# Small row loads on another queue, and a new order and PSUM tile in the first expert block of a streaming-encoder kernel

## The chip, the cores and the metric

The kernel runs on one core of one Trainium2 chip. Its metric is the time in microseconds that the device needs for one execution. Five engines work side by side and wait for one another by semaphores: TensorE (PE; its weight loads are shown apart as PEld), VectorE (DVE), ScalarE (ACT), GpSimd (POOL) and SyncE (SP), which only issues DMAs here. A suffix q (PEq, SPq) marks an engine's instructions that are not counted as busy: branches, loads of registers, DMA issues.

## The reference

For 512 tokens of width 1024, the reference does a LayerNorm, a token mixer (one projection, a gated MLP over blocks, a gated DeltaNet, a merge), a second LayerNorm, and then a mixture of 32 experts, behind which a third LayerNorm stands. The part that the change touches is the mixture:

```python
grp = argmax(softmax(x @ w_rg + b_rg))            # 1 of 4 groups
top_v, top_i = top_k(le, 2)                       # 2 of the group's 8 experts
gate = p_grp * softmax(top_v)
def expert_block(args):
    xb, e = args
    hb = silu(xb @ w1[e]) * (xb @ w3[e])
    return hb @ w2[e]
out = zeros.at[tok].add(y * gate)
h = layer_norm(DEEPNORM_ALPHA * h + out)
```

How many tokens an expert gets depends on the inputs, so the kernel learns it only while it runs.

## The kernel before, in words

Everything up to the router is one long stretch of TensorE work (projections in three passes of split float32). The router places every token: `place(t)` (L1279) runs for four tiles of 128 tokens, its products `cps` count the tokens of each expert, and its products `sps` (L1318) sort them. `sort` (L1325) turns these into indices. `units` (L1475) makes `cnti` from the counts, three integers for each expert, with three comparisons on `cps`, two operations and a cast (L1488). Before the change `units` is called in `place` for the last tile, between the operations that lead to `oh`.

**The experts.** The class `Experts` (L1517) streams the weights of 32 experts in an order that `ord` gives, 6 MB each: four chunks of 1 MB for `w1` and `w3` together and two for `w2`. `run` (L1555) makes a list `steps` of these chunks, and `load(n)` issues the next n of them by `load_big` (L465, the DMA at L472) on SyncE's queue into 17 buffers `raw` in turn; the first block's first chunk is put 14th in the list and goes into a tile of its own, `once`. Of the list, 18 chunks are issued ahead. Then three are issued after the first block's up products, four after each later block's, and two after each block's down products. Each waits until the readers of its buffer's last content are done, and for the semaphore lane that it gets: DMA issues from SyncE and ScalarE share eight lanes, DMAHW0 to 7, in the order of the program, those from GpSimd have others, DMASW0 to 7, and a DMA waits until the lane's last one has landed.

**A block.** Per expert, `up` (L1762) forms x @ w1 and x @ w3. It has a small part, `up(b, None)`, 32 rows `xs` with the weights' columns in four quarters, and large parts `up(b, 0)` and `up(b, 1)` of 64 rows each, in halves of the columns. Its loop over k takes eight slices of 128, two in each chunk, thus k0 and k1 read the first chunk, k2 and k3 the second. The large parts stand under `If` on the count (more than 32, more than 96), the second under the first. All products land in one PSUM tile `u` (L1537), whose last third is the small part's (`self.end`, L1538). `gate` (L1772) makes h = silu(u1) * u3, ScalarE's activation (L1783) and VectorE's product (L1784). `turn` (L1786) transposes h, `down` (L1797) multiplies with `w2`, `store_y` copies the result into `once` and GpSimd scatters it to `y_dram` (L1812). Blocks whose experts are known to be short have the small part alone (`short`). `n` (L1643) loads a count from `cnti` into a register of one engine (L1647) and keeps it.

**The first block** has code of its own, `first` (L1651), since its tokens come straight from the router. `run` first asks `If(n(0) > NA)` (L1600), NA being 64. Then `first` does the small products k0 to k3, the large parts' first half under `If(n > 32)` (L1663) and `If(n > 96)` (L1665), k4 and k5, the second half, then `gate(0, 0)` for the large part (L1670) and k6 and k7. If the count is over 64, the small rows were not the right ones; they are then copied by `tail_rows` and all small products are done again (L1672). The small part's gate follows in `run`, by `gate(b, 1)`.

**The tail's rows.** `Tail` prepares the last LayerNorm while experts run. At block 8 it calls `load_rows` (L1005): GpSimd clears `rx` (L1012), ScalarE's queue issues three DMAs of four rows each into it (L1014), GpSimd clears `rp` (L1015). Behind that GpSimd issues two gathers (L1918). `split_rows` (L1020) begins with a cast of `rx` on ScalarE (L1023).

## Time and profile before

| | |
|---|---|
| time, median of 3 runs | 1171.09 us (1170.65 to 1171.74) |
| profiled execution | 1168.46 us |
| its span | 1166.7 us |
| busy PE / DVE / ACT / POOL | 1030.9 / 631.0 / 367.4 / 214.5 us |
| mean granted clock of TensorE | 0.953 |
| bytes that the DMAs moved | 268.35 MB |

The profile is of one execution, which took 2.63 us less than the median of the runs, and its span is 1.8 us shorter than its own time. A row of a timeline gives the start in us, the duration in us, engine, line and operation, the tile written and the tile read, a count, and in brackets the idle time ahead of it with what ended it. Rows that belong together are put into one, so x16 is sixteen instructions. A row of waits gives the waiting queue, its releaser, the total in us, how often, and the longest. Windows give the busy time of each engine in a stretch. The granted clock is TensorE's, 1.00 being full. DMA share is the mean busy share of the core's 16 DMA engines, and a stream without gaps reads slightly over 1.

### The profile page before, as it was taken

How to read it: one execution, taken by the hardware profiler on the slowest of the kernel's cores; microseconds unless marked ns; L12 is line 12 of the kernel's file. 1: busy time of each engine (PE TensorE's matmuls, PEld its weight loads, DVE VectorE, ACT ScalarE, POOL GpSimd, SP SyncE). 2: the span in 40 equal slices, each digit the busy share in tenths (PEclk: the TensorE clock that was granted, in tenths of full speed). 3: DMA queues.
4: the chain of work that ended last, by engine and by line, in shares of the span. 5: the costliest groups of instructions: out<-in, count | busy, mean ns of one | idle time of the engine just before them, and what ended most of it. 6: DMA issues, size and time to landing. Idle time of an engine off the chain costs nothing. (4 is left out here: it accounts for less than half of the span.)

```text
span 1166.7 us, 18941 instructions
## 1 busy us (share of the span) xinstructions
PE 1030.9 (88%) x7046; PEld 683.4 (59%) x7046; DVE 631.0 (54%) x1420; ACT 367.4 (31%) x803; POOL 214.5 (18%) x288
## 2 busy tenths in 40 slices
PE   5999999999999999999999977797788787878754
PEld 4888788877777777777887733343334443333321
DVE  8475444477678776863585744353234433222256
ACT  6343356444544554544532121112111111010110
POOL 3010100132212222120100112223121222121110
PEclk9999999999999999999999989899899999998955
DMA  5412432611121121111737589998999999999996
GB/s 215 151 70 78 161 106 91 235 55 55 56 72 56 54 73 55 54 56 54 287 123 315 201 330 406 394 391 338 408 367 409 393 409 383 417 388 408 414 418 253
DMA packets 56138, 268.35 MB, mean 230 GB/s; under 512 B 10795, under 2 KB 15179, under 8 KB 32216
## 3 DMA queue, kind: packets, MB, share of 16 engines
q1 hardware_dynamic: 44400, 246.96, 55.2%
q0 software_dynamic: 9008, 14.82, 3.8%
q10 hardware_dynamic: 2616, 5.04, 1.2%
q8 instruction: 73, 1.20, 0.4%
q14 instruction: 41, 0.34, 0.1%
HBM read 273.74 MB, written 21.00 MB: 253 GB/s over the span
## 5 line engine op out<-in xcount | busy, mean ns | idle before, releaser
L275 PE MATMUL psi<-hTh,hi 128*128 128x512 f32 x448 | 183.8, 412 | 0.0
L275 PE MATMUL psi<-hTh,lo 128*128 128x512 f32 x448 | 179.9, 402 | 0.3 <-DVE lo L275 0.3
L275 PE MATMUL psi<-hTl,hi 128*128 128x512 f32 x448 | 179.7, 402 | 0.0
L1784 DVE TENSOR_TENSOR h<-h,u 128x128 f32<-128x128 f32 (+2 forms) x33 | 17.9, 542 | 250.6 <-ACT h L1783 245.1
L275 DVE TENSOR_TENSOR lo<-raw,hi 128x1024 fp32r<-128x1024 f32 x74 | 92.5, 1250 | 75.1 <-ACT hi L275 74.9
L1769 PE MATMUL u<-raw,xs 128*32 128x256 f32 x1296 | 88.9, 413 | 36.3 <-DMA raw<-in_w 22.6
L275 ACT CAST hi<-raw 128x1024 fp32r<-128x1024 f32 x74 | 77.4, 1046 | 107.3 <-PE psi L275 89.9
L275 PEld LDWEIGHTS psi<-hTl,hi 128*128 128x128 f32 x448 | 84.2, 188 | 20.6 <-issue 3.0
L275 PEld LDWEIGHTS psi<-hTh,hi 128*128 128x128 f32 x448 | 84.2, 188 | 20.2 <-issue 3.3
L275 PEld LDWEIGHTS psi<-hTh,lo 128*128 128x128 f32 x448 | 84.4, 188 | 18.4 <-issue 1.9
L1783 ACT ACTIVATE h<-u 128x128 f32<-128x128 f32 (+2 forms) x33 | 15.8, 480 | 243.1 <-PE u L1769 127.3
L1769 PEld LDWEIGHTS u<-raw,xs 128*32 128x32 f32 x1296 | 42.5, 116 | 77.9 <-DMA raw<-in_w 25.4
L1769 PE MATMUL u<-raw,x 128*64 128x512 f32 x304 | 72.9, 622 | 9.2 <-PEq L1681 7.1
L1812 POOL DMA_INDIRECT y_rows<-once,itail x28 | 25.3, 903 | 253.4 <-DVE once L1832 220.0
L275 DVE SCALAR_TENSOR_TENSOR acc<-xp,cols,acc 128x512 f32<-128x512 f32 x72 | 54.1, 751 | 5.3 <-ACT acc L275 4.3
L1793 ACT COPY hT<-t 128x128 f32<-128x128 f32 x32 | 8.5, 265 | 153.4 <-PE t L1790 146.6
L1769 PEld LDWEIGHTS u<-raw,x 128*64 128x64 f32 x304 | 23.1, 142 | 52.3 <-issue 50.3
L1832 DVE COPY once<-yz 32x256 f32<-32x256 f32 x112 | 46.7, 417 | 12.7 <-PE yz L1805 5.8
L1805 PE MATMUL yz<-raw,hT 128*32 128x256 f32 x576 | 43.1, 438 | 11.0 <-DMA raw<-in_w 9.1
L275 POOL TENSOR_TENSOR rk<-ssk,mhalf 128x4 f32<-128x4 f32 x8 | 10.0, 1249 | 178.0 <-DVE ssk L275 178.0
L1695 POOL DMA_INDIRECT mh<-h_dram,idx x36 | 35.0, 972 | 40.3 <-issue 26.5
L1805 PE MATMUL y<-raw,hT 128*64 128x512 f32 x160 | 38.0, 620 | 3.5 <-PEq L1681 2.6
(541 smaller groups left out, 1959.7 us busy)
## 6 DMA issues: line engine op xcount, KB each, us to landing
raw<-in_w SPq DMA_DIRECT2D x147, 1024.0 KB
raw<-in_wt SPq DMA_DIRECT2D x73, 512.0 KB
rawl<-in_w SPq DMA_DIRECT2D x22, 1024.0 KB
rawh<-in_w SPq DMA_DIRECT2D x22, 1024.0 KB
raw<-in_wv SPq DMA_DIRECT2D x8, 512.0 KB
y_rows<-zero SPq DMA_DIRECT2D x8, 512.0 KB
rawl<-in_wo SPq DMA_DIRECT2D x3, 1024.0 KB
vt<-in_x SPq DMA_DIRECT2D x4, 512.0 KB
```

Of the source, the lines that this page charges most:

```text
L275: op._ins = getattr(getattr(self.nc, op.attr), op.name)(*map(real, op.args), **{k: real(x) for k, x in op.kw.items()})
L1695: self.nc.gpsimd.indirect_dma_start(out=x, out_offset=None, in_=self.h1_dram, in_offset=bass.IndirectOffsetOnAxis(ap=self.blocks[b][2 + i] ...
L1769: self.nc.tensor.matmul(self.u[q * r:(q + 1) * r, NP if p is None else p, 0:c], x[:, k, r0:r0 + r], self.raw[b, k // 2][:, o:o + c], start ...
L1783: self.nc.scalar.activation(out=h, in_=u[:, :, 0], func=AF.Silu)
L1784: self.nc.vector.tensor_mul(out=h, in0=h, in1=u[:, :, 1])
L1793: self.nc.scalar.copy(out=x[:, n], in_=self.t[1][:, 0:128])
L1805: self.nc.tensor.matmul(y[q * r:(q + 1) * r, 0:c], t[:, i, j * r:(j + 1) * r], self.raw[b, 4 + k // 2][:, o:o + c], start=k == 0, stop=k == 3)
L1812: x = self.nc.gpsimd.indirect_dma_start(out=out, out_offset=bass.IndirectOffsetOnAxis(ap=idx, axis=0), in_=src, in_offset=None, bounds_che ...
L1832: nc.vector.tensor_copy(out=small[:, q], in_=src)
```

## The change

It has four parts. The three row loads of `load_rows` are issued by GpSimd in place of ScalarE. `units` is called in `sort` and no longer in `place`. The small part's products get a PSUM tile of their own, `us`, so `u` keeps the large parts only, and `gate` does its two parts as two operations on each engine. And the first block does k0 to k3 ahead of its first question for the count, then k4, loads block 1's counts, and does k5, the large part's gate, k6 and k7. The products done again for a count over 64 are k0 to k4 and stand inside the first half's `If`; the `k == end` of a redone k1 only closes a group ahead of them.

```diff
@@ load_rows
-            nc.scalar.dma_start(out=self.rx[32 * i:32 * i + 4], in_=self.a["rows"][R_L1G:R_L2B + 1, :])
+            nc.gpsimd.dma_start(out=self.rx[32 * i:32 * i + 4], in_=self.a["rows"][R_L1G:R_L2B + 1, :])
@@ place
-        if t == NT - 1:
-            a = self.eq.rearrange("p a b -> p (a b)").bitcast(F32)[:, 0:3 * E].rearrange("p (a b) -> p a b", a=3)
-            self.units(W, self.cps[:, NT], self.cnti, made, a)
@@ sort
+        a = self.eq.rearrange("p a b -> p (a b)").bitcast(F32)[:, 0:3 * E].rearrange("p (a b) -> p a b", a=3)
+        self.units(self.W, self.cps[:, NT], self.cnti, self.made, a)
@@ Experts.__init__
-        self.u = ps.tile([128, NP + 1, 512], F32, name="u")
-        self.end = self.u[:, NP]
+        self.u = ps.tile([128, NP, 512], F32, name="u")
+        self.end = ps.tile([128, 512], F32, name="us")
@@ run
         if clear:
+            self.up(0, None, range(0, 4))
             with self.tc.If(self.n(0) > NA):
                 self.s[0]["z"] = self.turn_late(0)
...
-                self.gate(b, 1 if clear and b == 0 else None)
+                self.gate(b, (1,) if clear and b == 0 else (1, 0))
@@ first
         self.s[0]["x"] = self.x[0]
+        up(0, None, range(4, 5))
+        self.n(1), self.n(1, ET.PE, 1)
         with If(d() > 32):
             self.affine(self.x[0], slice(0, NA), self.own(0))
             with If(d() > NA):
-                self.affine(self.x[0], slice(NA, NB), self.s[0]["z"], 3)
+                self.affine_late(0, self.s[0]["z"])
         self.affine(self.xs[1], slice(0, 32), self.own(1), 2)
         self.affine(self.x[1], slice(0, NA), self.own(1))
-        up(0, None, range(0, 4))
-        for h, ks in enumerate((range(4, 6), range(6, 8))):
+        for h in range(2):
             with If(n > 32):
+                if h == 0:
+                    with If(n > NA):
+                        up(0, None, range(1, 2), 1)
+                        up(0, None, range(0, 5))
                 up(0, 0, h)
                 with If(n > 96):
                     up(0, 1, h)
-            if h:
-                self.gate(0, 0)
-            up(0, None, ks)
-        with If(d() > NA):
-            self.tail_rows(0)
-        with If(n > NA):
-            up(0, None)
+            if h == 0:
+                up(0, None, range(5, 6))
+        self.gate(0, (0,))
+        up(0, None, range(6, 8))
@@ gate
-        self.nc.scalar.activation(out=h, in_=u[:, :, 0], func=AF.Silu)
-        self.nc.vector.tensor_mul(out=h, in0=h, in1=u[:, :, 1])
+        for part in (1,) if self.short(b) else parts:
+            if part:
+                h, u = self.s[b]["h"][:, n - 1], self.end[:, 0:256].rearrange("p (w n) -> p w n", w=2)
+                u, w = u[:, 0], u[:, 1]
+            else:
+                h = self.s[b]["h"][:, 0:n - 1]
+                u = self.u.rearrange("p a n -> p (a n)").rearrange("p (a w n) -> p a w n", a=n - 1, w=2)
+                u, w = u[:, :, 0], u[:, :, 1]
+            self.nc.scalar.activation(out=h, in_=u, func=AF.Silu)
+            self.nc.vector.tensor_mul(out=h, in0=h, in1=w)
```

Three places show how it moves instructions. In the rows below, names such as `raw_5447` are the buffers, and brackets name what an instruction waits for by semaphore lane.

The first place is the start of the first block on TensorE. Before, from the last sorting product to k3 (`once` holds the first chunk, `raw_5447` the second):

```order
L1318 MATMUL sps<-wt,oh 128x32
L1692 UNCONDITIONAL_BRANCH
L1647 TENSOR_LOAD cnti
L1600 COMPARE_AND_BRANCH
L1728 MATMUL y_5463<-ident,mh 128x96 x5
L1728 MATMUL y_5464<-ident,mh 128x96 x3
L1600 UNCONDITIONAL_BRANCH x2
L1692 UNCONDITIONAL_BRANCH
L1655 UNCONDITIONAL_BRANCH
L1769 MATMUL u<-once,xs_4776 32x256 x8
L1769 MATMUL u<-raw_5447,xs_4776 32x256 x8
```

The same place now, to k4 (`raw_5448` is the third chunk):

```order
L1316 MATMUL sps<-wt,oh 128x32
L1768 MATMUL us<-once,xs_4776 32x256 x8
L1768 MATMUL us<-raw_5447,xs_4776 32x256
L1695 UNCONDITIONAL_BRANCH
L1768 MATMUL us<-raw_5447,xs_4776 32x256 x7
L1648 TENSOR_LOAD cnti
L1601 COMPARE_AND_BRANCH
L1731 MATMUL y_5463<-ident,mh 128x96 x5
L1731 MATMUL y_5464<-ident,mh 128x96 x3
L1601 UNCONDITIONAL_BRANCH x2
L1695 UNCONDITIONAL_BRANCH
L1768 MATMUL us<-raw_5448,xs_4776 32x256 x4
```

The sixteen products of k0 to k3 moved ahead of the load of the count and its branch, and k4 stands behind the branch.

The second place is the end of the first block on TensorE. Before, from k6 to the first question of block 1 (`raw_5449` is the fourth chunk):

```order
L1769 MATMUL u<-raw_5449,xs_4776 32x256 [waits DMAHW3_49,DVE_49]
L1769 MATMUL u<-raw_5449,xs_4776 32x256 x7
L1670 UNCONDITIONAL_BRANCH
L1672 COMPARE_AND_BRANCH
L1769 MATMUL u<-once,xs_4776 32x256 [waits DVE_49]
L1769 MATMUL u<-once,xs_4776 32x256 x7
L1769 MATMUL u<-raw_5447,xs_4776 32x256 x8
L1769 MATMUL u<-raw_5448,xs_4776 32x256 x8
L1769 MATMUL u<-raw_5449,xs_4776 32x256 x8
L1672 UNCONDITIONAL_BRANCH
L1672 UNCONDITIONAL_BRANCH [waits PE_49]
L1647 TENSOR_LOAD cnti
```

The same place now, again from k6:

```order
L1768 MATMUL us<-raw_5449,xs_4776 32x256 [waits DMAHW3_49]
L1768 MATMUL us<-raw_5449,xs_4776 32x256 x7
L1750 COMPARE_AND_BRANCH
L1731 MATMUL y_5463<-ident,mh 128x96 [waits DMASW2_49,DMASW3_49,PE_49,Activation_49]
L1731 MATMUL y_5463<-ident,mh 128x96 x4
L1731 MATMUL y_5464<-ident,mh 128x96 [waits Activation_49]
L1731 MATMUL y_5464<-ident,mh 128x96 x2
```

The wait for VectorE (the large part's gate) at k6 is gone, and so is the redo of all small products behind it; block 1's late rows (under its own `If`) come next.

The third place is block 8, where the rows are loaded. Before, on ScalarE, from block 7's gate to block 8's and the cast of `rx`:

```order
L1783 ACTIVATE h<-u 128x640 [waits PE_49]
L1793 COPY hT<-t_4775 128x128 [waits PE_49,Activation_49]
L1795 COPY hT<-t_4774 128x512 [waits DVE_49,PE_49]
L1014 DMA rx<-in_rows 4x1024 [waits DMAHW2_49,Pool_49]
L1014 DMA rx<-in_rows 4x1024 [waits DMAHW3_49]
L1014 DMA rx<-in_rows 4x1024 [waits DMAHW5_49]
L1783 ACTIVATE h<-u 128x128 [waits PE_49]
L1023 CAST rp<-rx 96x1024 [waits DMAHW3_49,DMAHW5_49,DMAHW2_49,Pool_49]
```

The same loads now, on GpSimd, between a scatter, a gather, and the tail's gathers:

```order
L1812 DMA y_rows<-once,itail 1024x1024 [waits DMASW2_49,DVE_49]
L1698 DMA mh<-h_dram,idx 64x1024 [waits DMASW3_49,DMASW1_49,PE_49]
L1012 MEMSET rx 96x1024
L1014 DMA rx<-in_rows 4x1024 [waits DMASW4_49,Pool_49]
L1014 DMA rx<-in_rows 4x1024 [waits DMASW5_49]
L1014 DMA rx<-in_rows 4x1024 [waits DMASW6_49]
L1015 MEMSET rp 128x1024
L1918 DMA lgate<-gd_dram,lidx_5491 128x2 [waits DMASW7_49]
L1918 DMA x_5471<-h_dram,lidx 128x1024 [waits DMASW0_49,DVE_49]
```

The loads left ScalarE, where block 8's gate (128x128) stood behind them, and stand in GpSimd's queue between the two memsets, on its lanes. What that does to the weight loads' lanes on SyncE, before:

```order
L472 DMA raw_5447<-in_w 128x2048 [waits DMAHW0_49,PE_49]
L1681 UNCONDITIONAL_BRANCH
L1683 UNCONDITIONAL_BRANCH
L472 ISA
L472 DMA raw_5448<-in_w 128x2048 [waits DMAHW1_49,PE_49]
L472 ISA
L472 DMA raw_5449<-in_w 128x2048 [waits DMAHW2_49,PE_49]
```

And the same three loads now:

```order
L472 DMA raw_5447<-in_w 128x2048 [waits DMAHW5_49,PE_49]
L1684 UNCONDITIONAL_BRANCH
L1686 UNCONDITIONAL_BRANCH
L472 ISA
L472 DMA raw_5448<-in_w 128x2048 [waits DMAHW6_49,PE_49]
L472 ISA
L472 DMA raw_5449<-in_w 128x2048 [waits DMAHW7_49,PE_49]
```

The load into `raw_5449` waited for lane DMAHW2, the one that a row load on ScalarE had taken; now the lanes of the weight loads follow one another without a load of another engine between them.

More of the change, by code (lines that the diff above doesn't have):

```diff
@@ L1733, in affine_late @@
         self.affine(self.x[b % 2], slice(NA, NB), zs, 3)
-        self.tail_rows(b)
-    def tail_rows(self, b):
         self.nc.vector.tensor_copy(out=self.xs[b % 2], in_=self.x[b % 2][:, :, ds(self.n(b, ET.DVE, 2), 32)])
@@ L1760, in place, with up @@
         return (4, 0, 32) if p is None else (2, 64 * p, 64)
-    def up(self, b, p, h=None):
+    def up(self, b, p, h=None, end=KD - 1):
         x, (n, r0, r) = self.xs[b % 2] if p is None else self.s[b]["x"], self.place(p)
@@ L1768, in up, with gate @@
                 o = k % 2 * 1024 + q * c
-                self.nc.tensor.matmul(self.u[q * r:(q + 1) * r, NP if p is None else p, 0:c], x[:, k, r0:r0 + r],
-                                      self.raw[b, k // 2][:, o:o + c], start=k == 0, stop=k == KD - 1)
-    def gate(self, b, part=None):
+                self.nc.tensor.matmul((self.end if p is None else self.u[:, p])[q * r:(q + 1) * r, 0:c], x[:, k, r0:r0 + r],
+                                      self.raw[b, k // 2][:, o:o + c], start=k == 0, stop=k == end)
+    def gate(self, b, parts=(1, 0)):
         n = 2 * NP + 1
-        u = self.u.rearrange("p a n -> p (a n)")[:, 0:256 * n].rearrange("p (a w n) -> p a w n", a=n, w=2)
-        if not part:
+        if "h" not in self.s[b]:
             self.s[b]["h"] = self.hp.tile([128, n, 128], F32, name="h")
-        h = self.s[b]["h"]
-        if self.short(b):
-            part = 1
-        if part is not None:
-            sl = slice(n - 1, n) if part else slice(0, n - 1)
-            h, u = h[:, sl], u[:, sl]
-        self.nc.scalar.activation(out=h, in_=u[:, :, 0], func=AF.Silu)
-        self.nc.vector.tensor_mul(out=h, in0=h, in1=u[:, :, 1])
+        for part in (1,) if self.short(b) else parts:
[8 more added lines that the diff above has]
+            self.nc.vector.tensor_mul(out=h, in0=h, in1=w)
     def turn(self, b):
```

## The prediction

> **What bounds the kernel now.** I read the page's slices first, then the chain of waits in order of time, then windows over the expert stage.
>
> ```profile
> DMA  5412432611121121111737589998999999999996
> ```
>
> From the 24th of the 40 slices (29.2 us each) on, thus from about 670 us, the DMA engines are busy nearly without a break: that is the expert stage, and what stands before it is TensorE's, which no edit touches. The chain shows what the end waits for:
>
> ```profile
> 1126.83 26.65 DMA raw<-in_w
> ...
> 1161.60 1.01 POOL out L1912
> ```
>
> The chain is DMA up to the last weight chunk at 1153.48, then a tail of 13.2 us to the span's end at 1166.7 that no edit touches. So the end moves only if the stream of weights ends earlier, and with its bytes fixed it ends earlier only by holes in it that close. The windows (us, then busy time of PE, PEld, DVE, ACT, POOL with counts, granted clock, DMA share, GB/s) show the holes:
>
> ```profile
> 682.00:688.00 6.00, 1.87 (x22) 0.74 (x20) 2.79 (x17) 1.71 (x4) 1.09 (x2) 0.76 0.48 135
> 688.00:692.00 4.00, 4.00 (x12) 1.31 (x10) 1.17 (x10) 0.00 (x0) 1.80 (x2) 0.51 0.91 334
> 785.00:797.00 12.00, 10.16 (x117) 4.74 (x108) 5.68 (x14) 2.57 (x5) 6.66 (x7) 1.00 0.71 249
> 850.00:870.00 20.00, 16.02 (x125) 6.46 (x119) 5.54 (x13) 1.52 (x4) 6.71 (x7) 0.91 0.95 352
> 870.00:1000.00 130.00, 105.14 (x1116) 50.71 (x1114) 53.21 (x108) 15.47 (x35) 29.93 (x32) 0.97 1.02 399
> ```
>
> A full stream reads 1.02. Against that, **hole A** in block 0 is 6 x (1.02 - 0.48) + 4 x (1.02 - 0.91) = 3.2 + 0.4 = 3.7 us of lost transfer; **hole B** in block 8 is 12 x (1.02 - 0.71) = 3.7 us; **hole C**, 850 to 870, is 20 x 0.07 = 1.4 us; no edit touches what stands there, so it counts for the low end only. After 870 there is none. All that can be won is 3.7 + 3.7 + 1.4 = 8.8 us, and each microsecond won in a hole is one at the end as long as nothing later uses it up. Over 0.2% (2.3 us) is what a measurement of this kernel tells from no change.
>
> **Hole A: the first block's order.** Who holds the weight queue there (SyncE's queue: waits with total, times, longest; then its issues)?
>
> ```profile
> SPq L472 <- PEq L1672: 9.5, 1, 9.5
> ```
>
> ```profile
> 685.47 0.33 SPq L472 DMA_DIRECT2D raw<-in_w  x1
> ```
>
> The load after the first 18 goes into the buffer of the first block's second chunk (k2, k3), and that is given free only at the end of the second `If(n > NA)` (L1672), at 685.47. What TensorE does until then:
>
> ```profile
> 677.88 0.21 PE L1318 MATMUL sps<-wt,oh 128*128 128x32 f16 x2 [0.18 <-DVE oh L1315]
> 679.02 1.07 PE L1769 MATMUL u<-once,xs 128*32 128x256 f32 x16 [0.93 <-PEq L1600]
> 679.88 1.07 PE L1769 MATMUL u<-raw,xs 128*32 128x256 f32 x16
> 681.12 1.07 PE L1769 MATMUL u<-raw,xs 128*32 128x256 f32 x16 [0.17 <-PEq L1663]
> 684.22 1.12 PE L1769 MATMUL u<-raw,xs 128*32 128x256 f32 x16 [2.02 <-DVEq L1670]
> 687.45 5.86 PE L1769 MATMUL u<-raw,x 128*64 128x512 f32 x16 [2.11 <-PEq L1681]
> ...
> 801.02 3.65 PE L1769 MATMUL u<-raw,x 128*64 128x512 f32 x16 [1.19 <-PEq L1681]
> ```
>
> Only products of 32 rows run in block 0, none of 64: its count is small and the large part is skipped. Three idle times stand in a chain: 0.93 for the count, 2.02 because the last small products (k6, k7) write the PSUM tile that the large part's gate still reads, 2.11 for two more counts, which block 1 asks for. The changed order removes them one by one (block 1's counts are loaded ahead of the first `If` now).
>
> (1) *k0 to k3 before the count.* They need only `xs` and the first chunks, not the count, so they follow the sorting products at once: 677.88 + 0.21 = 678.09 as it stands.
>
> ```profile
> 675.04 0.20 DVE L1488 CAST cnti<-oeq 128x96 int32<-128x96 f32 x1
> ```
>
> ```profile
> L1647 PEldq TENSOR_LOAD <-cnti x3: 308/320/492, 677.9 to 686.4; - x3
> ```
>
> The count's six DVE operations, by the row of their last at most 0.20 us each, 1.2 in all, now stand behind `xs` and `oh`. Those come sooner by what six overlapping operations take, for which I put 0.7 us, so k0 starts near 677.4 instead of 679.02. Behind them the count is written by 677.3 + 1.2 = 678.5 at the latest, and after a load of 0.32 to 0.49 it is there by 679.0. The products k0 to k3 last 679.88 + 1.07 - 679.02 = 1.9 us, thus until 679.3. So the later count costs nothing: these products cover it, with 0.3 us to spare. Without the cover TensorE would wait 1.6 us. Pool and DVE load their count later too, but the large parts for which they need it are skipped in block 0.
>
> (2) *Their own PSUM tile.* k6 and k7 no longer wait for the gate of the large part; the 2.02 us go. What follows 679.3 is the count's branch (0.93 at its dearest, as above), k4 (a quarter of the 2.1 us that two groups of 1.07 take: 0.5) and an empty `If` (0.17): it closes near 680.9 instead of 685.47, and nothing that reads the second chunk stands behind it, since the redo with k0 to k4 lies inside. Thus the held load leaves 4.6 us earlier. The next two leave behind k5 and the second `If`, near 681.6, and behind k6 and k7 (1.12), near 682.7. At a full stream's 399 GB/s a chunk (128 x 2048 x 4 bytes, 1.05 MB) lasts 2.6 us, so these three carry it from 682, where the share falls, to 689.8.
>
> (3) *Block 1* needs the gate of block 0's large part, because that reads `u`:
>
> ```profile
> 681.46 1.28 ACT L1359 ACT_TABLE_LOAD   x1
> ...
> 682.86 0.58 ACT L1783 ACTIVATE h<-u 128x512 f32<-128x512 f32 x1
> ```
>
> ```profile
> 683.47 0.69 DVE L1784 TENSOR_TENSOR h<-h,u 128x512 f32<-128x512 f32 x1 [1.41 <-ACT h L1783]
> ```
>
> ScalarE comes to it through its table loads, which stay, so the gate still ends at about 683.47 + 0.69 = 684.2, and that, hidden before behind 687.45, is now what is late: block 1 starts at about 684.1 to 684.2, 3.3 us earlier. If its first half takes 3.65 us, loads go on by 688, before 689.8: the hole closes, 3.7 us, or 3.1 if the first load still comes 0.6 late. If it takes 5.86 us as now, the next load leaves near 690.1; the rows show that a load needs about 2 us until the stream is full (issues from 685.47, still 0.91 after 688), so some 1.7 us of the hole come back: 2.0 us.
>
> Which of the two hangs on the granted clock: 0.76 and 0.51 in the two windows, and 5.86 us there for what took 3.65 at 801. Both lengths are rows of this kernel, and of the 5.1 us of idle time ahead of block 1 about 1.5 stay, so I take the middle of 2.0 and 3.7: **A = 2.8 us**. [...]
>
> **Hole B: the rows' loads.** Around 777 to 792 SyncE's queue (first), ScalarE and GpSimd read:
>
> ```profile
> 776.88 0.33 SPq L472 DMA_DIRECT2D raw<-in_w  x1
> ```
>
> ```profile
> 792.42 2.85 SPq L472 DMA_DIRECT2D raw<-in_w  x4
> ```
>
> ```profile
> 788.78 1.94 ACTq L1014 DMA_DIRECT2D rx<-in_rows  x3
> 790.77 0.28 ACT L1783 ACTIVATE h<-u 128x128 f32<-128x128 f32 x1 [5.88 <-DMA rx<-in_rows]
> 792.76 1.05 ACT L1023 CAST rp<-rx 96x1024 bf16<-96x1024 f32 x1 [1.72 <-DMA rx<-in_rows]
> ```
>
> ```profile
> 787.79 0.97 POOL L1012 MEMSET rx<- 96x1024 f32 x1
> ...
> 791.17 1.00 POOL L1918 DMA_INDIRECT x<-h_dram,lidx  x1 [0.31 <-issue]
> 795.89 0.90 POOL L1812 DMA_INDIRECT y_rows<-once,itail  x1 [3.72 <-DVE once L1832]
> ```
>
> SyncE issues nothing for 15.2 us. By the order of the program its next load waits for semaphore lane DMAHW2 (the quoted rows of the change), which the rows' load on ScalarE holds; that waits for GpSimd's memset of `rx`, which ends at 787.79 + 0.97 = 788.76, and is issued at 788.78. SyncE goes on at 792.42, when they have landed, and issues four loads in 2.85 us: their buffers had long been free. So a transfer of 48 KB, behind a memset that GpSimd reaches late, holds the 1 MB weight loads. After the change the three loads have lanes of GpSimd's own, and the weight loads' lanes follow one another (HW5, 6, 7, 0). The stall goes; what is next is the freeing of buffers by TensorE, which the four loads at once show to be early. I take 3.7 less 0.2 for the first load's own start: **B = 3.5 us**. ScalarE's 5.88 us before its gate L1783 goes too; it lies beside the stream.
>
> *What it adds.* GpSimd issues three DMAs; its own rows show 0.90 to 1.00 us for one, so 3.0 us, against 0.65 each (1.94 / 3) on ScalarE. GpSimd's queue behind them holds the memset of `rp`, two gathers, then block 7's scatter at 795.89, before which it idles 3.72 us: hidden, with 0.7 to spare. The cast at 792.76 waits for `rx`; `rp` is used only after the splits of blocks 9 and 10. If the idle time were gone the 3.0 us would delay the scatter, and through `once` the next block's copies.
>
> **The split gate.** Large and small part are two operations per engine now.
>
> ```profile
> 699.88 0.71 ACT L1783 ACTIVATE h<-u 128x640 f32<-128x640 f32 x1
> ```
>
> ```profile
> L1784 DVE TENSOR_TENSOR h<-h,u 128x640 f32<-128x640 f32 x15 | 12.3, 821 | 178.4 <-ACT h L1783 178.4
> L1784 DVE TENSOR_TENSOR h<-h,u 128x128 f32<-128x128 f32 x17 | 4.9, 288 | 70.8 <-ACT h L1783 65.3 <-issue 5.4
> ```
>
> With the rows above for 128x512 (0.58 on ScalarE, 0.69 on VectorE) and 128x128 (0.28 and 0.29): 0.58 + 0.28 - 0.71 = 0.15 us and 0.69 + 0.29 - 0.82 = 0.16 us more in each of 15 blocks: 15 x 0.31 = 4.6 us in all. They lie beside a full stream, and behind the up products TensorE has the down products of the block before to do. Taken as 0; without that cover it is 4.6.
>
> **Sum.** 2.8 + 3.5 = 6.3 us off the profiled execution's 1168.46 gives 1162.2. The median of the runs lies 2.63 us above that execution, so the forecast is 1171.09 - 6.3 = **1164.8**.
>
> **The rivals.** (a) *Only the rows' part acts*: the first `If` closes as late as before, since the later count, or the gate through its table loads, holds TensorE by some 4 us: 1171.09 - 3.5 = 1167.6. For it speaks the thin cover of 0.3 us in (1); against it that the held load no longer stands behind the gate.
> (b) *Only the first block's part acts*: SyncE is held at 777 by something else that the lane hid: 1171.09 - 2.8 = 1168.3. Against it speak the four loads at once.
> (c) *TensorE becomes the bound later.*
>
> ```profile
> 868.72 0.34 SPq L472 DMA_DIRECT2D rawl<-in_w  x1
> 872.59 0.34 SPq L472 DMA_DIRECT2D rawh<-in_w  x1
> ```
>
> ```profile
> 820.12 1.94 PE L1769 MATMUL u<-rawh,xs 128*32 128x256 f32 x16 [2.59 <-DMA rawh<-in_w]
> ```
>
> At 868.72 to 872.59 SyncE waits 3.5 us for buffers and the stream stays full, so at least 3.5 us were queued. A stream 6.3 us ahead of an unmoved TensorE would run dry for 6.3 - 3.5 = 2.8 us, or 4.8 with a load's 2 us start: 1167.6 to 1169.6. Against it: at 820.12 TensorE itself waits 2.59 us for a weight, so it moves forward with the stream.
> (d) *It doesn't do what it says*: other waits of the same length stand behind both: 1171.1.
> (e) *Slower: GpSimd's queue.* Its DMAs on plain rows are not in the trace at this place. The price decides: the three must last over 3.7 (idle) + 6.3 (gained) + 2.3 (the bound) = 12.3 us, 4.1 each; at 5 us each the scatter of block 7 is 11.3 us late, `once` with it, the copies, TensorE's next products and the buffers: 15 - 3.7 - 6.3 = 5 us slower, 1176.1. The rows of 0.90 to 1.00 speak against it. [...]
>
> **How the numbers follow.** Both holes close 0.60 (1164.8); (a) 0.14; (b) 0.08; (c) 0.07, its range lying on both sides of the bound at 1168.75, so 0.03 faster and 0.04 the same; (d) 0.06; (e) 0.05. Faster: 0.60 + 0.14 + 0.08 + 0.03 = 0.85; the same 0.10; slower 0.05. The low end is all three holes, 1171.09 - 8.8 = 1162.3, rounded down to 1162.0 for the spread of the runs; the high end takes in (a) and (b), 1168.3, and the half of (c) up to 1168.8. Left out are (d), (e) and the other half of (c), 0.15.
>
> **What would show it.** Right: the first load after the 18 leaves near 681; k6 and k7 follow without the 2.02; block 1 starts near 684; no gap of SyncE from 777 to 792; DMA share 1.0 in both stretches; the last weight chunk lands near 1147. Clock: 3.65 or 5.86 us for block 1's first products tells A's size. Wrong: a wait of TensorE on `cnti` at 678, a weight load still behind a semaphore of `rx`, rows' loads over 3 us each on GpSimd, or a new hole between 800 and 875 with SyncE waiting for TensorE.

## The result and the profile after

The changed kernel takes 1162.51 us in the median of six runs (1161.37 to 1166.76); the kernel before, run beside it, takes 1170.92 (six runs). The ratio is 0.9941 with a 95% interval of 0.9923 to 0.9959, that is 6.9 us less (4.8 to 9.0), where 6.3 were forecast (the medians alone lie 8.4 us apart). A second set of six runs gave a median of 1163.32 and a ratio of 0.9950 (0.9935 to 0.9966), 5.9 us less. Two runs of kernels below, one of b_clear_five (2527 us) and one of a_ask_first (2012 us), took 1.7 to 2.2 times as long as all the others and are left out of the ratios.

The two profiled executions differ by less, 1168.46 against 1165.03 us, and this must be cleared first. Windows of the kernel before, far ahead of anything that the change touches:

```profile
500.00:600.00 100.00, 97.19 (x510) 77.51 (x509) 61.88 (x108) 47.64 (x89) 13.12 (x18) 1.00 0.42 149
```

The same window of the changed kernel:

```profile
500.00:600.00 100.00, 97.18 (x497) 77.15 (x496) 58.18 (x104) 46.10 (x87) 12.10 (x18) 0.97 0.42 148
```

The mean granted clock was 0.97 in place of 1.00, with the same code. The mean hides a short stretch at half clock:

```profile
531.60:538.20 6.60, 6.60 (x23) 4.86 (x23) 0.00 (x0) 0.78 (x3) 0.00 (x0) 0.50 0.24 79
```

That is 6.6 x (1 - 0.50) = 3.3 us lost, and by that this execution comes late to the place of the change. The last router operation that both order alike (L1284) is the mark from which to compare. Before, on VectorE:

```profile
672.93 0.19 DVE L1284 TENSOR_TENSOR M<-mk 128x32 bf16<-128x32 f32 x1
```

And after, with the count's cast further down:

```profile
676.23 0.19 DVE L1284 TENSOR_TENSOR M<-mk 128x32 bf16<-128x32 f32 x1
...
681.13 0.21 DVE L1488 CAST cnti<-oeq 128x96 int32<-128x96 f32 x1
```

The mark lies 3.30 us later. From the mark to the span's end it is 1166.7 - 672.93 = 493.8 us before and 1163.2 - 676.23 = 487.0 after, 6.8 us less, which agrees with the runs. The changed kernel's profile in the second set (after_again) has its mark at 672.80, without that stretch, and 1161.1 - 672.80 = 488.3 us behind it, 5.5 less. Two executions of one kernel thus differ by 1.3 us behind the mark. Times are set against this mark where two kernels are compared, unless they are given as they stand in the rows.

The chain of waits still ends in the stream of weights (DMA from 1123.86 for 25.61 us), and goes on:

```profile
1149.47 0.04 issue
1149.51 1.98 PE us L1805 x16
```

The last chunk lands 1149.47 - 676.23 = 473.24 us behind the mark, before it was 1153.48 - 672.93 = 480.55, 7.3 us later. The tail grew by half a microsecond, as the last products now take 1.98 us, where they took 1.11 (granted clock 0.50 for 1.00). The windows over the stream:

```profile
682.00:688.00 6.00, 2.73 (x40) 0.87 (x32) 3.49 (x10) 4.55 (x9) 2.07 (x2) 1.00 0.97 351
688.00:692.00 4.00, 3.50 (x10) 1.21 (x12) 2.68 (x21) 0.00 (x0) 0.77 (x1) 0.57 1.01 342
785.00:797.00 12.00, 11.31 (x145) 5.61 (x137) 7.21 (x18) 1.13 (x3) 7.56 (x10) 1.00 1.03 381
850.00:870.00 20.00, 15.91 (x98) 5.90 (x98) 5.23 (x12) 2.41 (x7) 5.82 (x6) 0.91 0.97 363
```

Holes A and B are closed, 0.97 to 1.03 where 0.48, 0.91 and 0.71 stood. Hole C stands, but not where it was. In steps of 10 us from the mark, the one with the lowest share there begins 180 us behind it before, and 170 us behind it in the changed kernel and in after_again:

```profile
852.93:862.93 10.00, 7.38 (x55) 2.96 (x57) 3.91 (x8) 1.24 (x3) 3.67 (x4) 0.98 0.91 324
846.23:856.23 10.00, 7.34 (x61) 3.08 (x61) 4.10 (x9) 1.52 (x4) 2.83 (x3) 0.98 0.87 344
842.80:852.80 10.00, 9.52 (x120) 4.52 (x112) 6.32 (x15) 0.67 (x2) 0.96 (x2) 1.00 0.78 301
```

Against 1.02 that is 1.1, 1.5 and 2.4 us of lost transfer: the hole comes 10 us sooner and takes 0.4 to 1.3 us back.

Share alone says too much, though. A window of 12 us laid 8 us behind the mark shows hole A in bytes. Before:

```profile
681.00:693.00 12.00, 7.75 (x48) 2.70 (x48) 4.92 (x28) 2.69 (x7) 3.89 (x4) 0.72 0.71 245
```

After:

```profile
684.00:696.00 12.00, 8.12 (x46) 2.85 (x48) 4.85 (x27) 2.57 (x7) 3.40 (x4) 0.86 0.98 330
```

The share gained 12 x 0.27 = 3.2 us, but the bytes only 12 us x 85 GB/s = 1.02 MB, which a full stream of 399 GB/s moves in 2.6 us. GpSimd's queue moved about as much in both windows (0.36 and 0.38 MB); before, part of it ran in the hole, now it shares the stream. The weights' own queue went from 2.54 to 3.54 MB. In block 8 the bytes gained are 12 us x (381 - 249) GB/s = 1.58 MB, 4.0 us. Together 6.6 us.

The first block on TensorE after:

```profile
680.30 0.21 PE L1316 MATMUL sps<-wt,oh 128*128 128x32 f16 x2 [0.16 <-DVE oh L1313]
680.45 1.07 PE L1768 MATMUL us<-once,xs 128*32 128x256 f32 x16
681.34 1.05 PE L1768 MATMUL us<-raw,xs 128*32 128x256 f32 x16
682.71 0.64 PE L1768 MATMUL us<-raw,xs 128*32 128x256 f32 x8 [0.33 <-PEq L1601]
684.14 0.64 PE L1768 MATMUL us<-raw,xs 128*32 128x256 f32 x8 [0.79 <-PEq L1665]
684.95 1.07 PE L1768 MATMUL us<-raw,xs 128*32 128x256 f32 x16 [0.17 <-PEq L1665]
688.50 5.32 PE L1768 MATMUL u<-raw,x 128*64 128x512 f32 x16 [2.48 <-DVE den L1365]
```

The products follow the sorting at once, the branch on the count costs 0.33, k6 and k7 no longer wait 2.02. But block 1 starts at 12.3 us behind the mark, where 11.2 were forecast, and its first products still take 5.32 us, for 5.86 before. SyncE's held loads after:

```profile
684.12 3.42 SPq L472 DMA_DIRECT2D raw<-in_w  x3
```

The first leaves 7.9 us behind the mark (before: 685.47 - 672.93 = 12.5), 4.65 us earlier.

Block 8, ScalarE and then GpSimd after:

```profile
791.13 0.28 ACT L1783 ACTIVATE h<-us 128x128 f32<-128x128 f32 x1 [3.81 <-PE t L1745]
800.03 1.04 ACT L1023 CAST rp<-rx 96x1024 bf16<-96x1024 f32 x1 [8.62 <-DMA rx<-in_rows]
```

```profile
791.47 1.63 POOL L1014 DMA_DIRECT2D rx<-in_rows  x3 [0.29 <-POOL rx L1012]
...
796.95 0.90 POOL L1812 DMA_INDIRECT y_rows<-once,itail  x1 [0.30 <-issue]
802.00 1.04 POOL L1812 DMA_INDIRECT y_rows<-once,islot  x1 [4.15 <-ACT once L1837]
```

A new wait stands here: the last row load is out by 793.10, and the cast gets the rows only at 800.03, 6.9 us later (before, 792.76 - 790.72 = 2.0 us from the last issue to the cast), beside a stream with a DMA share of 1.03 there, where 0.71 stood. ScalarE is held 8.62 us by it, and the large scatters come 4.15 us later for that.

### The profile page after: what moved, and what is told of

The parts are those of the page before. It is cut to its first block, busy times and chain, and to the rows that moved or that the text cites. A ratio compares the mean times of both kernels' runs of the same rounds, so it can differ in the third digit from the quotient of the medians.

```text
span 1163.2 us, 18964 instructions
## 1 busy us (share of the span) xinstructions
PE 1033.1 (89%) x7046; PEld 684.4 (59%) x7046; DVE 633.9 (54%) x1435; ACT 369.2 (32%) x818; POOL 215.5 (19%) x291
## 5 line engine op out<-in xcount | busy, mean ns | idle before, releaser
L1768 PE MATMUL us<-raw,xs 128*32 128x256 f32 x1296 | 90.1, 418 | 33.5 <-DMA raw<-in_w 24.0
L1784 DVE TENSOR_TENSOR h<-h,us 128x128 f32<-128x128 f32 x32 | 9.2, 288 | 191.7 <-ACT h L1783 181.2
L1768 PEld LDWEIGHTS us<-raw,xs 128*32 128x32 f32 x1296 | 42.6, 117 | 75.9 <-issue 25.5
L1783 ACT ACTIVATE h<-us 128x128 f32<-128x128 f32 x32 | 8.9, 277 | 187.2 <-PE us L1768 118.2
```

The lines of the kernel that those rows point to most:

```text
L1768: self.nc.tensor.matmul((self.end if p is None else self.u[:, p])[q * r:(q + 1) * r, 0:c], x[:, k, r0:r0 + r], self.raw[b, k // 2][:, o:o ...
L1783: self.nc.scalar.activation(out=h, in_=u, func=AF.Silu)
L1784: self.nc.vector.tensor_mul(out=h, in0=h, in1=w)
```

## The experiments

Theory: the gain is the sum of two closed holes in the stream of weights, A by the first block's order and tile, B by the lane that the row loads held; nothing between takes them back. Rivals: one part brings it all, the split gate or GpSimd's queue takes some back, or it is only a matter of which engine issues. The kernel before was run beside each set, the changed kernel beside the last one; the ratios below are against the kernel before.

**b_rows_gpsimd**: the kernel before with this edit alone.

```diff
-            nc.scalar.dma_start(out=self.rx[32 * i:32 * i + 4], in_=self.a["rows"][R_L1G:R_L2B + 1, :])
+            nc.gpsimd.dma_start(out=self.rx[32 * i:32 * i + 4], in_=self.a["rows"][R_L1G:R_L2B + 1, :])
```

> The kernel before with the three row loads issued by GpSimd and nothing else. Theory (the lane that the row loads take holds the weight loads): the gap of SyncE from 777 to 792 goes, the DMA share in block 8 rises from 0.71 to about 1, hole A stays; 3.5 us faster, ratio 0.9970. Rival (GpSimd's queue or the slower landing of the rows takes it back): within 1 us of before. Rival (hole B was TensorE's all along): the gap of SyncE stays.

Measured: 0.9969 (0.9956 to 0.9982), 3.6 us faster. Windows over holes A and B:

```profile
682.00:688.00 6.00, 4.44 (x48) 2.11 (x48) 2.77 (x7) 4.44 (x8) 2.07 (x2) 0.75 0.71 264
688.00:692.00 4.00, 1.55 (x18) 0.65 (x20) 2.23 (x16) 0.28 (x1) 0.00 (x0) 0.98 0.48 143
785.00:797.00 12.00, 11.38 (x155) 5.99 (x149) 7.92 (x20) 1.13 (x3) 7.22 (x9) 1.00 1.02 382
```

B is closed (1.02), A stands (0.71 and 0.48, this execution being 2.9 us later). From the mark (675.86) to the span's end it is 490.1 us, 3.7 less than before, as in the runs. The theory holds.

**a_rows_scalar**: the changed kernel with the edit undone.

```diff
-            nc.gpsimd.dma_start(out=self.rx[32 * i:32 * i + 4], in_=self.a["rows"][R_L1G:R_L2B + 1, :])
+            nc.scalar.dma_start(out=self.rx[32 * i:32 * i + 4], in_=self.a["rows"][R_L1G:R_L2B + 1, :])
```

> The changed kernel with the row loads back on ScalarE's queue. Theory: hole B is back (a gap of SyncE of some 15 us around block 8, DMA share near 0.7 for 12 us), hole A stays closed; 3 to 3.5 us faster than before, ratio 0.9972, and about as much slower than the changed kernel. Rival (the two parts overlap, and one alone brings nearly all): 5 us or more faster than before.

Measured: 0.9974 (0.9956 to 0.9992), 3.0 us faster. The same windows:

```profile
682.00:688.00 6.00, 2.40 (x27) 0.93 (x29) 4.04 (x19) 2.96 (x7) 1.94 (x2) 0.96 0.99 328
688.00:692.00 4.00, 4.00 (x14) 1.52 (x12) 1.19 (x10) 0.00 (x0) 1.81 (x2) 0.63 1.04 320
785.00:797.00 12.00, 11.02 (x137) 5.36 (x129) 7.00 (x17) 2.17 (x4) 6.00 (x6) 1.00 0.63 226
```

A is closed, B is back and larger than before, 12 x (1.02 - 0.63) = 4.7 us for 3.7. By the runs the parts add: 0.9969 x 0.9974 = 0.9943, beside 0.9941 and 0.9950. But the interval of this kernel reaches from 0.9 to 5.1 us, and its trace doesn't show the 3.0. SyncE's first issue behind the gap:

```profile
793.49 0.33 SPq L472 DMA_DIRECT2D raw<-in_w  x1
```

That is 118.9 us behind its mark (674.62), where before has 792.42 - 672.93 = 119.5, and from there to the end both take 374.3 us: only 0.6 us are gained (493.2 for 493.8). The weights' queue had moved 10.10 MB in the first 30 us behind the mark, for 8.85 before, but 41.14 MB in the first 120, for 41.05. The lead was used up at hole B, since that gap ends when GpSimd comes to the memset and the rows have landed, and the row loads came no sooner (116.2 us behind the mark for 115.9). In this trace A brings little as long as B stands; with B closed it brings 490.1 - 487.0 = 3.1 us (b_rows_gpsimd against the changed kernel).

**b_clear_vector** and **b_clear_five**: the kernel before, its row loads on ScalarE as they were, but the memset ahead of them done by another engine, or five times over.

```diff
-        nc.gpsimd.memset(self.rx[0:96], 0.0)
+        nc.vector.memset(self.rx[0:96], 0.0)
```

> The kernel before, row loads still on ScalarE, but rx is cleared by VectorE, which comes to it at 785.3, in place of GpSimd at 787.8. Theory (the lane is held until the memset is done and the rows have landed): the row loads leave some 2.5 us earlier (near 786.3), SyncE's gap ends some 2.5 us earlier, about 2.5 us faster, ratio 0.9979. Rival (what matters is which engine issues, not when): no change, 0.999 to 1.001.

```diff
-        nc.gpsimd.memset(self.rx[0:96], 0.0)
+        for _ in range(5):
+            nc.gpsimd.memset(self.rx[0:96], 0.0)
```

> The kernel before with the clearing of rx on GpSimd done five times over, four memsets of 0.97 us more. Theory: the row loads leave 3.9 us later, SyncE's gap grows by 3.9 us, and the time by nearly as much, 3 to 3.9 us slower, ratio 1.0030. Rival (the lane is not what holds SyncE): GpSimd's 3.9 us lie in its idle time, no change.

Measured: 0.9995 (0.9980 to 1.0010) and 1.0011 (0.9996 to 1.0025). Both are less than the theory's number, and neither can be told from no change by time alone. The queues tell why. The row loads of b_clear_vector on ScalarE, then SyncE's last issue ahead of the gap and the first behind it:

```profile
786.58 1.16 ACTq L1014 DMA_DIRECT2D rx<-in_rows  x3
```

```profile
774.05 0.33 SPq L472 DMA_DIRECT2D raw<-in_w  x1
788.56 0.33 SPq L472 DMA_DIRECT2D raw<-in_w  x1
```

The same of b_clear_five:

```profile
793.38 1.33 ACTq L1015 DMA_DIRECT2D rx<-in_rows  x3
```

```profile
782.27 0.33 SPq L472 DMA_DIRECT2D raw<-in_w  x1
796.90 0.33 SPq L472 DMA_DIRECT2D raw<-in_w  x1
```

The gap's end follows the row loads in every kernel that has them on ScalarE: 788.56 for loads at 786.58, 792.42 for 788.78, 793.49 for 790.78 (a_rows_scalar), 796.90 for 793.38, thus 2.0 to 3.6 us behind. That is the lane: in the trace of before the load at 792.42 waits for the semaphore that the row load issued at 788.78 signals. But its begin moved too: in these two programs the row loads hold lanes DMAHW1, 2 and 4, and DMAHW3, 5 and 6, where before they hold 2, 3 and 5. So SyncE is stopped one load (2.6 us) sooner in the one and later in the other. The gap ended 3.9 us sooner with 2.6 us less queued, a net 1.3 (0.6 measured), and 4.5 us later with 2.6 us more queued, a net 1.9 (1.3 measured). The size expected was wrong; the mechanism stands by the queues, not by the times.

**b_own_tile**: the kernel before with the tile and the gate of the changed one, and nothing else of it.

```diff
-        self.u = ps.tile([128, NP + 1, 512], F32, name="u")
-        self.end = self.u[:, NP]
+        self.u = ps.tile([128, NP, 512], F32, name="u")
+        self.end = ps.tile([128, 512], F32, name="us")
...
-                self.gate(b, 1 if clear and b == 0 else None)
+                self.gate(b, (1,) if clear and b == 0 else (1, 0))
...
-                self.gate(0, 0)
+                self.gate(0, (0,))
... (`up` and `gate` write and read the two tiles as in the change)
```

> The kernel before with the small part's own PSUM tile and the split gate, but with its own order in the first block (count first, all redone products behind k7) and its row loads on ScalarE. Theory: k6 and k7 no longer wait 2.02 us for the gate, so the first held load leaves about 2 us earlier after the last count operation (10.5 us behind the operation that makes M for the last tile, L1284, where before has 12.5 and the changed kernel 7.9), hole A shrinks by 2 us, and the time by 1.5 to 2 us, ratio 0.9985. Rival (the tile alone brings nothing, since the load still stands behind the second If): 12 us or more, no change of time. Rival (the split gate costs what it takes, 4.6 us): slower, 1.002 or more.

Measured: 0.9983 (0.9971 to 0.9995), 2.0 us faster. TensorE there:

```profile
681.97 1.94 PE L1769 MATMUL us<-once,xs 128*32 128x256 f32 x16 [0.93 <-PEq L1600]
683.65 1.70 PE L1769 MATMUL us<-raw,xs 128*32 128x256 f32 x16
685.53 1.07 PE L1769 MATMUL us<-raw,xs 128*32 128x256 f32 x16 [0.18 <-PEq L1663]
686.77 1.07 PE L1769 MATMUL us<-raw,xs 128*32 128x256 f32 x16 [0.17 <-PE us L1769]
```

The wait of 2.02 us ahead of k6 and k7 is down to 0.17, and the split gate does not cost the rival's 4.6 us. The held load leaves at 687.99, 12.1 us behind the mark (675.88), not 10.5, which taken alone is the sign of the rival that the tile brings nothing: in this execution the first products ran at half clock (1.94 and 1.70 us for 1.07; granted clock 0.50 from 681.6 to 684.9). Another execution of the old order had that too: in b_rows_gpsimd the mean granted clock was 0.75 from 682 to 688, and the load left 13.6 us behind the mark. Against that one it is 1.5 us. As in a_rows_scalar, the row loads are on ScalarE in this kernel, and from the mark to the end its trace has 1169.2 - 675.88 = 493.3 us, 0.5 less than before; the 2.0 us rest on the runs (0.6 to 3.4).

**a_ask_first**: the changed kernel with k0 to k3 behind the question again.

```diff
-            self.up(0, None, range(0, 4))
             with self.tc.If(self.n(0) > NA):
...
-        up(0, None, range(4, 5))
+        up(0, None, range(0, 5))
```

> The changed kernel with k0 to k3 behind the first question for the count, as before, all else kept. Theory: the later count is no longer covered; k0 starts 1.5 to 2 us behind the sorting products' end instead of at once, the first held load leaves 9.5 to 10 us behind L1284's last operation instead of 7.9, and 0.5 to 1.5 us of hole A come back: 0.9948 of before, where the changed kernel has 0.9941. Rival (the order of count and products matters little since the stream has more ahead than the windows show): load later, no hole, same time as the changed kernel.

Measured: 0.9936 (0.9918 to 0.9953), which can't be told from the changed kernel's 0.9941. TensorE and the window 8 to 20 us behind the mark (673.15):

```profile
679.46 1.49 PE L1767 MATMUL us<-once,xs 128*32 128x256 f32 x16 [2.02 <-DVEq L1657]
```

```profile
681.00:693.00 12.00, 9.38 (x72) 3.75 (x66) 4.78 (x27) 2.71 (x7) 3.46 (x4) 0.90 0.85 300
```

The uncovered count costs 2.02 us, and the held load leaves 10.5 us behind the mark in place of 7.9 (9.5 to 10 expected; the granted clock was 0.50 from 680.1 to 683.2). By share 12 x (0.98 - 0.85) = 1.6 us of the hole come back, by bytes 12 us x 30 GB/s = 0.36 MB, 0.9 us. But this doesn't last: 60 us behind the mark the weights' queue has moved 21.54 MB, for 21.63 in the changed kernel and 20.54 before. Block 1's first products took 3.65 us here (from 686.75, at a granted clock of 1.00) and end 17.3 us behind the mark, for 17.6 in the changed kernel with its 5.32 us. So the order moves the load as the prediction said, and in these two traces nearly nothing of it is left in the stream. Whether it would bring something with the same clock is open.

**a_count_early**: the changed kernel with the call of `units` back in `place`. **a_block1_late**: the changed kernel without the early loads of block 1's counts. Both were run once (1163.40 and 1163.68 us), for the trace.

```diff
+        if t == NT - 1:
+            a = self.eq.rearrange("p a b -> p (a b)").bitcast(F32)[:, 0:3 * E].rearrange("p (a b) -> p a b", a=3)
+            self.units(W, self.cps[:, NT], self.cnti, made, a)
...
-        a = self.eq.rearrange("p a b -> p (a b)").bitcast(F32)[:, 0:3 * E].rearrange("p (a b) -> p a b", a=3)
-        self.units(self.W, self.cps[:, NT], self.cnti, self.made, a)
```

> The changed kernel with the count's six operations back in place, ahead of oh and xs. Theory: the sorting products end 0.9 us later after L1284 (5.2 us as before, 4.3 in the changed kernel), the branch on the count no longer waits (0.33 us in the changed kernel), and the first held load leaves about 0.5 us later. Rival: no shift, VectorE's six operations run beside what oh waits for.

```diff
-        self.n(1), self.n(1, ET.PE, 1)
```

> The changed kernel without the early loads of block 1's counts; they come behind k6 and k7 again. In the changed kernel the branch to block 1's rows (L1750) takes 2.61 us, while a transfer on the instruction queue runs, and block 1 starts 12.3 us behind L1284. Theory (the branch waits for its code to come, and that is asked for only by the branch): the loads of 0.3 us each and their branches come on top, block 1 starts at 13 us or later. Rival (the code comes at its own time, and the loads run beside it): the branch is short, and block 1 starts at 12.3 again.

In a_count_early k0 starts at 679.27, 5.1 us behind the mark (674.18) against 4.2, the branch's wait is 0.18 for 0.33, and the load leaves at 682.73, 8.55 behind the mark for 7.9: 0.65 us later, as the theory had it. In a_block1_late the branch ahead of block 1 is still long (3.09 us, the table at the end). Block 1 starts 13.0 us behind the mark there (685.82 - 672.84), 0.7 later, as the theory expected. But this doesn't decide for it. Only one of the two loads stands ahead of that branch, which begins no later than in the changed kernel (8.58 us behind the mark for 8.78) and ends at 11.67 for 11.39; the second load and its wait, 0.4 us, come behind it. The rest of the 0.7 is the branch's end, and that lies between 11.4 and 11.8 in the table's first four rows wherever the branch begins.

**after_again**, **a_pool_late**, **a_rows_sync** and **a_cast_later** are the last set, on one chip.

> The changed kernel once more, beside the three kernels of this set, so that they can be set against it on the same chip: 0.9941 of before, within 0.9923 to 0.9959.

Measured: 0.9950 (0.9935 to 0.9966), a little less gained than in the first set.

In a_pool_late GpSimd's queue is 3.9 us longer behind the row loads:

```diff
-        nc.gpsimd.memset(self.rp, 0.0)
+        for _ in range(5):
+            nc.gpsimd.memset(self.rp, 0.0)
```

> The changed kernel with the clearing of rp on GpSimd, behind the row loads, done five times over: 3.9 us more in GpSimd's queue ahead of block 7's scatters. In the changed kernel GpSimd has only 0.3 us of idle time left ahead of the small scatter, and 4.15 ahead of the large ones. Theory (the queue has a cover further down, since the large scatters wait for ScalarE's copies anyway and the weight stream is full): within 0.1% of the changed kernel. Rival (the forecast's slower case begins here, the scatter and once come late, TensorE with them): 3 us or more slower than the changed kernel, 0.9967.

Measured: 0.9944 (0.9927 to 0.9960), no change. GpSimd there:

```profile
790.99 5.00 POOL L1016 MEMSET rp<- 128x1024 bf16 x5
...
800.10 1.03 POOL L1813 DMA_INDIRECT y_rows<-once,islot  x1 [0.34 <-ACT once L1838]
```

The idle time of 4.15 us ahead of the large scatters is down to 0.34: the additional 4 us lie in ScalarE's new wait. The slower case of the forecast has not begun at this price.

a_rows_sync puts the row loads on the third queue that could take them:

```diff
-            nc.gpsimd.dma_start(out=self.rx[32 * i:32 * i + 4], in_=self.a["rows"][R_L1G:R_L2B + 1, :])
+            nc.sync.dma_start(out=self.rx[32 * i:32 * i + 4], in_=self.a["rows"][R_L1G:R_L2B + 1, :])
```

> The changed kernel with the row loads on SyncE's own queue, among the weight loads. In the order of the program they stand nine weight loads further on than on ScalarE, at a place that SyncE reaches when the memset of rx is done. Theory (only a lane that waits for a memset not yet done stops the stream): no gap, the same time as the changed kernel, 0.9941. Rival (any row load on these lanes makes the hole): hole B back, 0.997 or more.

Measured: 1.0026 (1.0011 to 1.0040), slower than before, and 0.76% of before above the changed kernel in the same set (0.9950). This theory fell, and so did the rival as I put it: block 8 itself has no hole. SyncE, ScalarE, TensorE and the windows:

```profile
795.79 6.00 SPq L1014 DMA_DIRECT2D rx<-in_rows  x3
```

```profile
813.82 1.04 ACT L1023 CAST rp<-rx 96x1024 bf16<-96x1024 f32 x1 [26.20 <-DMA rx<-in_rows]
```

```profile
815.08 3.64 PE L1805 MATMUL yz<-raw,hT 128*32 128x256 f32 x32 [10.44 <-ACT hT L1793]
```

```profile
797.00:821.00 24.00, 11.89 (x81) 5.10 (x81) 4.48 (x7) 4.18 (x8) 4.30 (x4) 0.72 1.01 413
821.00:870.00 49.00, 38.82 (x361) 17.31 (x355) 18.77 (x39) 7.30 (x16) 10.72 (x12) 0.92 0.86 338
```

The memset is long done, but each of the three loads waits for a weight load to land (7.7 us in three waits, the longest 2.7), the last leaves at 801.54, and the rows land by 813.8. ScalarE's cast waits 26.2 us for them, the copy of h behind it holds TensorE for 10.44 us, the buffers come free late (SyncE waits 17.0 us for TensorE's from 790 to 875), and the stream starves afterwards: 49 x (1.02 - 0.86) = 7.8 us, where hole C made 1.4. So the new wait of ScalarE, harmless at 8.62 us, seems to decide at 26; this chain is read from the waits and was not cut by an edit.

a_cast_later takes that wait away from the changed kernel:

```diff
-        elif (b, at) in ((8, 3), (9, 3), (10, 3)):
-            kk.split_rows(b - 8)
+        elif (b, at) in ((9, 3), (10, 3)):
+            for i in range(2 if b == 9 else 1):
+                kk.split_rows(i if b == 9 else 2)
```

> The changed kernel with the cast of rx on ScalarE one block later (block 9 in place of 8), so that ScalarE doesn't wait 8.6 us for the rows, which land late in the full stream. Theory (the end hangs on the stream of weights, which is full there): ScalarE's wait goes, the time stays, 0.9941. Rival (the wait holds the transposed h and the copies to once, and by them TensorE and the buffers): 1 to 3 us faster than the changed kernel, 0.992 to 0.993.

Measured: 0.9942 (0.9928 to 0.9957). ScalarE there no longer waits for rows in block 8:

```profile
795.45 0.27 ACT L1793 COPY hT<-t 128x128 f32<-128x128 f32 x1 [6.58 <-PE t L1790]
```

The time stays: 8.62 us of ScalarE are beside the stream. No version of these beats the changed kernel by more than the runs can tell.

## Why the prediction was right

- **What bounds it.** The end hangs on the stream of weights, and only closed holes count: 7.3 us of landing and 6.8 us of the time from the mark to the end went (5.5 in after_again), the runs say 6.9 and 5.9. The ratio makes 1164.2 of 1171.09, beside the forecast of 1164.8; the median, 1162.51, lies in the range of 1162.0 to 1168.8, but only 0.5 us above its low end.
- **The sum of the two.** The prediction took each microsecond won in a hole as one at the end as long as nothing later uses it up. In the trace of a_rows_scalar something does: hole B, which ends when GpSimd's memset and the row loads are done, however far the stream is, leaves 0.6 us of hole A's gain. So the sum holds for both edits together, in which B is closed, and not for A alone, whose 1168.3 in rival (b) this trace doesn't bear out.
- **Hole A, forecast 2.8 us.** In the changed kernel it brought 2.6 us in bytes, and 3.1 us from the mark to the end on top of B's part; alone, 3.0 in the runs (0.9 to 5.1) and 0.6 in the trace. Of the steps, k0 sooner by 0.7 (measured 0.9 for the sorting products), a held load 4.6 us sooner (4.65) and a covered count (0.33 us left) came out. Two did not. Block 1 was to start with the end of the gate, at 11.2 us behind the mark; it started at 12.3, since the branch to its rows took 2.61 us, and the gate had been done 1.3 us earlier (its product at 686.46 lasts 0.69, to 687.15). And a slow first product of block 1 was to give 1.7 us of the hole back. It took 5.32 us, the next load left only 17.7 us behind the mark, and yet the share over that stretch was 0.98: the three loads lasted longer than the 7.8 us reckoned for them at 399 GB/s, as the weights' queue moved 3.54 MB in those 12 us, 295 GB/s, while GpSimd's queue took 10.7% of the DMA engines' time, 1.3 us. The middle of 2.0 and 3.7 was thus right by its size and not by its reason.
- **The clock.** That the idle time left ahead of block 1 bears on the clock, and so on the choice between 3.65 and 5.86 us, was the author's estimate; no run shows that it sets the clock. In the trace of the changed kernel it was halved right behind the longest idle time there, 2.48 us:

```profile
685.00:688.40 3.40, 1.02 (x16) 0.42 (x16) 1.58 (x8) 1.59 (x4) 0.95 (x1) 1.00 0.93 287
688.60:691.80 3.20, 3.20 (x8) 1.00 (x10) 2.13 (x17) 0.00 (x0) 0.56 (x1) 0.50 1.03 351
```

  In the kernel before, the 5.1 us of idle time ahead of block 1 are three pieces of 0.93, 2.02 and 2.11 us with products between, and the clock read 0.50 from 685.20 on, ahead of the third. So it was halved behind idle stretches of 2.0 and 2.5 us in these two; but in b_own_tile the same products took 3.65 us behind 2.12 us of idle time. What sets the clock, these runs don't show.
- **Hole B, forecast 3.5 us.** Alone it brought 3.6 in time and 3.7 from the mark to the end, and in the changed kernel 4.0 in bytes. The chain from memset to row loads to lane to weight load holds in each of four kernels (2.0 to 3.6 us from the row loads to the weight load behind them). The price on GpSimd was 3.0 us at 1.00 each, and measured 1.63 for three; the landing, not the issue, grew: 6.9 us, and ScalarE waits 8.62 for it. The landing was the gap in the prediction. a_cast_later shows that it cost nothing here, a_rows_sync, that the stream loses some 8 us where the same wait is three times as long.
- **The split gate, taken as 0.** b_own_tile has it and is faster by 2.0 us, where 1.5 to 2 were expected without any cost: the 4.6 us are hidden.
- **The rivals.** (a), only the rows' part acts, is excluded by the 3.1 us that A adds to it; (b), only the first block's, by b_rows_gpsimd. (c), TensorE as the later bound, is seen in small: hole C comes 10 us sooner and is 0.4 to 1.3 us larger, with SyncE waiting 4.6 us for TensorE's buffers there in both profiles of the changed kernel. The forecast took hole C as untouched. (e) did not begin at 3.9 us more in GpSimd's queue; its point of 12.3 us wasn't tried. The row loads on SyncE came out at 1.0026, on GpSimd at 0.9950 in the same set, and the three issues took 1.63 us on GpSimd for 1.94 on ScalarE in the kernel before: what decided was which queue and which lanes the small loads stand in, not how fast one is issued.
- **Still open.** Whether k0 to k3 ahead of the count bring anything by themselves: their 0.9 us of bytes in the hole are gone 60 us later, and the runs can't tell a_ask_first from the changed kernel. And what A is worth with B open: 3.0 us by the runs, 0.6 by the one trace.

## What to carry to other kernels

In the kernel before, a small load that waited for something late held the next load on its semaphore lane, and with it all that stood behind in that load's queue (15.2 us without an issue of SyncE). So give such a load lanes (an engine's queue) that the big stream doesn't use, and look for the gap in the issuing queue, not at the engine. Then ask when it lands: here it was 6.9 us behind its issue beside a stream at 1.03, for 2.0 us at 0.71, and whoever waits for it in order must not be one that TensorE waits for (10.44 us of TensorE in a_rows_sync). Where two holes in a stream are closed, reckon the gain in bytes over a window from a common mark; the share of busy engines also counted what else was moved (3.2 us of hole A by share, 2.6 by bytes). And ask what ends the later hole: if it is not the stream, the gain of the earlier one can be lost there, as in the trace of a_rows_scalar, where 0.6 us of it were left.

## What was not expected of the hardware

One branch took long. Branches of TensorE's queue in the first block of the kernel before take 0.07 to 0.43 us, but the one that leads to block 1's rows took 2.61, 3.12, 3.09, 2.06 and 1.33 us in the changed kernel, a_rows_scalar, a_block1_late, a_count_early and a_ask_first. From the transfers of the queue that the profile calls instruction, with times from the mark:

```
kernel          branch starts  takes   ends    instruction transfer near it
after               8.78       2.61    11.39   8.98, 0.94 us
a_rows_scalar       8.70       3.12    11.82   9.32, 0.94 us
a_block1_late       8.58       3.09    11.67   9.18, 1.01 us
a_count_early       9.45       2.06    11.51   9.10, 0.99 us
a_ask_first        11.39       1.33    12.72  10.30, 0.95 us
```

A 16 KB transfer on that queue lies near each, and the two branches that begin last, at 9.45 and 11.39, are the shortest; in the first four rows the branch ends at 11.4 to 11.8 wherever it begins. Whether a branch waits for that transfer was not shown. In the last two rows the transfer begins first, and the kernel before has one at 9.10 too, with no such branch near it. There, questions and loads of 0.2 to 0.4 us stood at that place, and no branch was long.

The other surprise is the clock. In the same code, far ahead of the change, TensorE ran at half clock for a few microseconds in some executions and not in others. From 530 to 540 us the mean granted clock was 1.00 in before, after_again and a_ask_first, 0.83 in a_rows_scalar, a_count_early and a_rows_sync, and 0.66 in the changed kernel, b_rows_gpsimd and b_own_tile. Against the mark of before these come 1.7, 1.3 and 1.3 us later in the second group (10 x 0.17 = 1.7) and 3.3, 2.9 and 3.0 in the third (10 x 0.34 = 3.4). That is up to half of what the change brings, and a part of the 5 us over which single executions spread. Why it falls there in some executions is open.
